# A two-layer hybrid decoder trunk: another order of chunks and engines, other first loads, smaller clears

## Chip, cores, metric

One Trainium2 chip, one core of it. The time is that of the whole kernel on the device in microseconds (us); a figure for a kernel is the median of its runs.

## What is computed

Two layers over 256 tokens of width 1024. One wide projection feeds two groups: HGRN2, a gated linear recurrence, and native sparse attention (compressed, selected and window keys). Their gated outputs go through `w_out`; then a second gated addition follows. The reference, cut:

```
for i in range(DEPTH):                                   # DEPTH = 2
    proj = rmsnorm(h, norm_g[i]) @ w_in[i]
    (hq, hf, hi, hgo, hz, nq, kcm, vcm, ksl, vsl, kwn, vwn, ngate, nz) = split(proj)
    log_f = logaddexp(log(lb), log1p(-lb) + log_sigmoid(hf)); k = (1 - lb) * sigmoid(-hf)
    o_hg  = rmsnorm(hgrn2(hq, log_f, k, hi))             # S_t = f_t S_(t-1) + k_t v_t; o_t = S_t q_t
    y_hg  = o_hg * sigmoid(hgo) * silu(hz)
    qn    = rmsnorm(nq)                                  # 8 heads of 64; q_rope = rope(qn)
    kc    = rmsnorm(compress(kcm)); vc = compress(vcm)   # 15 blocks of 32 tokens: silu(x @ w1) @ w2
    o_cmp = softmax(qn @ kc.T) @ vc
    o_slc = attention over the best selection blocks (4 blocks, all of them taken), k = rope(rmsnorm(ksl))
    o_win = window attention (window 512 over 256 tokens), k = rope(rmsnorm(kwn))
    y_nsa = (g0 * o_cmp + g1 * o_slc + g2 * o_win) * silu(nz)
    h = h + concat(y_hg, y_nsa) @ w_out[i]
    h = h + sigmoid(rmsnorm(h) @ w_pg[i]) * (p[i] @ w_pp[i])
```

## The kernel before

**Matrix products.** Every weight and every activation is split into a rounded part `hi` and a rest `lo`, and each product is three matmuls: hi by hi, hi by lo, lo by hi (`proj`, L581). A main matmul is 128x128 by 128x256; there are 2400. Weights come in chunks of 256 columns by 1024 rows, 1 MB each (the chunk `kk` has 280 columns), on SP's DMA queue (L426; ACT's queue L425 for the first two pieces) into four buffers `raw`. A chunk is cut into quarters: ACT casts `hi` (L534; for the first two chunks DVE may, L536), then DVE (L543) or GpSimd, called POOL (L544), subtracts for `lo`. A quarter is 128x512; nine pairs of such buffers exist. A chunk on PE is 48 main matmuls; its result lies in one of three PSUM banks `mm` (four more, `ax`, serve everything else, one, `po`, the attention sums) and is taken out by a function for each chunk (`ev_hf`, `ev_hi`, ...). The chunk names are those of the reference (`hf0`, `hf1` are the halves of hf, `cm` both compressed inputs, `kk` keys and gates, `vv` the values).

**Work beside the products.** The recurrence is a binary tree over time: elementwise scalings of tQ and tK on DVE and POOL (L420, L421), products by level on PE (L810 small levels, L870, L924), a masked copy L823 behind each L810, then L946 and L947. Compression (`ev_cm`): tqn (L991, L994), adds of the position term into PT (L420), the product with `w1` (L1022), an ACT step to t (L1028), L1037, then L1060 and L1061, L1067, L1092. Keys: roped by small steps of L420 or L421, scaled (POOL, L1246), rotated by a PE transposition (L1253), copied into tkh and tkl (L1261, L1264). Queries: L1131 to L1191, L1163 on PE. The softmax of the compressed keys: scores L1305, L1310 to L1344 on DVE, transposition L1351, result tPCh on ACT and tPCl on DVE (L1357), used by L1388. Attention runs in eight units a layer: scores L1426 and L1427, masked maximum on DVE (L1435), exponential on ACT (L1440), scaling on POOL (L1460), transposition on PE (L1477), copy on ACT (L1484) or DVE (L1481), sum L1402.

**Order.** No engine's order is written by hand. `Sched.run` is a greedy planner that runs when the kernel is built: all work is in threads; in each step the thread with the smallest start time plus `WGT[engine]` times its priority goes next. Priorities stand in `PRI`, the choice between engines (`alt`) is by the earlier end plus a bias in `PREF`, `STAY` lets PE stay with small products, durations are those written at each `op`, and `Port` marks DVE operations that the planner keeps apart from POOL's. What the chip does is then fixed: each engine runs its row in order and waits on semaphores.

The lines that the diff touches:

## Time and profile before

| | us |
|---|---|
| median of 3 runs | 386.61 (386.41 to 386.72) |
| profiled execution, its own time | 386.33 |
| its span in the trace | 384.4 |
| PE busy in the span | 375.0 |
| DVE busy | 310.5 |
| ACT busy | 260.6 |
| POOL busy | 114.0 |

The granted clock of PE is 0.999 over the span, 2.4 GHz. All engines run side by side; busy shares are means over a span whose stages differ, so the rows further down go by stage. Line numbers are those of the kernel before; in the changed kernel the same lines stand 5 to 8 lines further down (L543 is L548 there, L420 is L426, L924 is L932, L1028 is L1036, L1357 is L1365, L1426 is L1434).

### The profile page before, as it was taken

Reading aid. Unit: us, or ns where it says so; the run is one execution under the profiler, and the core shown is the slowest. Engines: PE = TensorE matmul, PEld = TensorE weight load, DVE = VectorE, ACT = ScalarE, POOL = GpSimd, SP = SyncE. Lnnn points to the kernel's source line nnn. Section 1 sums busy time; section 2 is a strip of 40 time slices with the busy share of each in tenths; the row PEclk is TensorE's granted clock in tenths of the full one; section 3 lists DMA queues with packets and bytes.
Section 4 is the critical chain, followed back from the end, with each engine's and each line's share of the span. In section 5 each row is a group of like instructions: output and inputs, shape, how many; then the busy total and the mean of one; then the engine's idle time right before and its main releaser. Section 6 shows DMA issues by size and latency. Waiting matters only on the chain.

```text
span 384.4 us, 9516 instructions
## 1 busy us (share of the span) xinstructions
PE 375.0 (98%) x3681; PEld 362.6 (94%) x3681; DVE 310.5 (81%) x791; ACT 260.6 (68%) x611; POOL 114.0 (30%) x135
## 2 busy tenths in 40 slices
...
GB/s 282 412 393 236 197 327 172 165 113 120 214 43 200 112 111 74 147 113 220 228 152 177 219 142 225 293 113 158 172 113 137 111 120 101 112 112 109 2 55 56
DMA packets 12286, 63.03 MB, mean 164 GB/s; under 512 B 1616, under 2 KB 2768, under 8 KB 5584
## 3 DMA queue, kind: packets, MB, share of 16 engines
...
HBM read 61.36 MB, written 1.05 MB: 162 GB/s over the span
## 4 chain that ended last, share of the span: by engine, by line
PE 75%; DVE 15%; DMA 5%; issue 2%; ACT 1%; POOL 0%; SPq 0%; POOLq 0%; ACTq 0%; DVEq 0%
PE mm L581 58%; DMA raw<-w_in 5%; PE po L1402 3%; PE mm L1612 3%; PE ax L1477 3%; DVE lo L543 3%; DVE PT L420 2%; PE ax L1426 2%; PE ax L810 1%; PE ax L1427 1%; DVE tK L420 1%; DVE tq L1191 1%; DVE tQ L420 1%; DVE t L1499 1%; PE po L1388 1%
## 5 line engine op out<-in xcount | busy, mean ns | idle before, releaser
L581 PE MATMUL mm<-xh,hi 128*128 128x256 f32 x608 | 175.5, 289 | 0.5 <-DVE hi L536 0.4
L581 PE MATMUL mm<-xl,hi 128*128 128x256 f32 x608 | 171.1, 281 | 0.0
L581 PE MATMUL mm<-xh,lo 128*128 128x256 f32 x608 | 170.6, 281 | 0.0
L534 ACT ACTIVATE hi<-raw 128x512 fp32r<-128x512 f32 (+1 forms) x203 | 123.4, 628 | 51.9 <-PE mm L581 38.3
L543 DVE TENSOR_TENSOR lo<-raw,hi 128x512 fp32r<-128x512 f32 (+2 forms) x183 | 125.7, 704 | 25.0 <-ACT hi L534 24.2
L581 PEld LDWEIGHTS mm<-xh,hi 128*128 128x128 f32 x608 | 114.4, 188 | 3.8 <-issue 1.4
L581 PEld LDWEIGHTS mm<-xh,lo 128*128 128x128 f32 x608 | 115.0, 189 | 0.4
L581 PEld LDWEIGHTS mm<-xl,hi 128*128 128x128 f32 x608 | 114.6, 188 | 0.4
L581 PE MATMUL mm<-hi,xh 128*128 128x256 f32 (+1 forms) x192 | 55.2, 288 | 0.0
L581 PE MATMUL mm<-lo,xh 128*128 128x256 f32 (+1 forms) x192 | 54.2, 282 | 0.2 <-DVE lo L543 0.2
L581 PE MATMUL mm<-hi,xl 128*128 128x256 f32 (+1 forms) x192 | 54.0, 281 | 0.0
L544 POOL TENSOR_TENSOR lo<-raw,hi 128x512 fp32r<-128x512 f32 x26 | 36.7, 1416 | 57.4 <-ACT hi L534 57.4
L1460 POOL TENSOR_SCALAR P<-P,s 128x128 f32<-128x128 f32 (+1 forms) x64 | 38.6, 618 | 34.3 <-DVE s L1453 18.5
L581 PEld LDWEIGHTS mm<-lo,xh 128*128 128x128 f32 x192 | 36.1, 188 | 0.4 <-DVE lo L543 0.4
L581 PEld LDWEIGHTS mm<-hi,xh 128*128 128x128 f32 x192 | 36.1, 188 | 0.4
L581 PEld LDWEIGHTS mm<-hi,xl 128*128 128x128 f32 x192 | 36.2, 188 | 0.0
L1440 ACT ACTIVATE P<-P,s 128x128 f32<-128x128 f32 (+1 forms) x64 | 28.3, 445 | 0.9 <-DVE s L1435 0.9
L1435 DVE CUSTOM_DVE_ANT_0 P<-ax,cn 128x128 f32<-128x128 f32 (+1 forms) x64 | 20.0, 351 | 4.2 <-PE ax L1427 3.2
L630 POOL TENSOR_TENSOR s<-s,mhalf 128x2 f32<-128x2 f32 x4 | 3.8, 946 | 55.8 <-DVE s L626 55.8
L1484 ACT ACTIVATE PT<-ax 128x512 f32<-128x512 f32 x24 | 14.0, 596 | 3.2 <-PE ax L1477 3.1
L1227 POOL TENSOR_TENSOR s<-s,mhalf 128x4 f32<-128x4 f32 x4 | 4.4, 1110 | 38.7 <-DVE s L1223 38.7
L1477 PE MATMUL ax<-cn,P 128*128 128x128 f32 x96 | 13.9, 272 | 0.0
...
## 6 DMA issues: line engine op xcount, KB each, us to landing
...
```

The source lines that it names most:

```text
L420: return alt([("V", dV2(n), lambda: V.tensor_tensor(out, in0, in1, op=fn), 0.0), ("G", dG2(n), lambda: G.tensor_tensor(out, in0, in1, op=f ...
L534: ("S", dS(m), lambda: S.activation(hi, src, AF.Copy), 0.0)]
L543: yield alt([("V", dV2(m), lambda: V.tensor_tensor(lo, src, hv, op=OP.subtract), 0.0), ("G", dG2(m), lambda: G.tensor_tensor(lo, src, hv, ...
L544: ("G", dG2(m), lambda: G.tensor_tensor(lo, src, hv, op=OP.subtract), PREF["lo_G"])],
L581: PE.matmul(out, lhsT=a, rhs=b, start=k == 0 and i == 0 and (j == 0 or nb == 2), stop=k == NK - 1 and i == 2, skip_group_check=True)
L1402: PE.matmul(po.ap[64 * par:64 * par + 64, tt * 128:(tt + 1) * 128], lhsT=vn[:, st, b, par], rhs=PTs[tt][par][b * (tt + 1) + st], start=Fal ...
L1435: yield op("V", dV(ns) + 0.02, lambda: V.tensor_tensor_reduce(P[:, b], sv[:, b], cn[:, CN_CA + 128 - ns + 128:CN_CA + 256], -1.0, 3.0e38, ...
L1440: yield op("S", Act("exp", dS(ns, 2)), lambda: S.activation(P[:, b], P[:, b], AF.Exp, bias=nm.ap[:, b:b + 1], scale=-1.0, accum_out=sm_.ap ...
L1460: ("G", dG(ns) + 0.05, lambda: G.tensor_scalar(P[:, b], P[:, b], w, 1.0, op0=OP.mult, op1=OP.mult), PREF["P_G"]),
L1477: PE.transpose(tb.ap[:, i * 128:(i + 1) * 128], Ps[par][1][:, b, st * 128:(st + 1) * 128], idf)
L1484: ("S", dS(w_), lambda: S.activation(PT.ap[:, 0:w_], tb.ap[:, 0:w_], AF.Copy), PREF["PT_S"])],
L1612: PE.matmul(out, lhsT=x[:, k, w], rhs=y[:, t], start=k == 0 and i == 0, stop=k == 1 and i == 2)
```

## The change

Four things change at once.

1. The planner's numbers: order of the chunks, `WGT`, `PREF`, `PRI`, `STAY`, the place of `w1` in the loads (behind the eighth chunk, not the fifth) and some durations. Tables are now kept for each layer, with equal entries. The arithmetic stays the same.
2. The clears of the five PT buffers cover only the columns 30 and 31 of each 32, not all 512.
3. The first loads: the small columns `sm` leave the first load of `h` and go on ACT's queue; of the first two weight pieces only the second stays on ACT's queue.
4. `lo` and other steps that two engines may do land elsewhere, since the bias is another.

```diff
-ORDER = ["hf0", "hi1", "hi0", "hq0", "kk", "cm", "hf1", "hq1", "nq0", "hgo0", "nq1", "vv", "hz0", "hz1", "nz1",
-         "hgo1", "nz0"]
+ORDER = [["hi0", "hi1", "hf0", "hq0", "kk", "cm", "hf1", "hq1", "nq0", "hgo0", "nq1", "hz0", "vv", "hz1",
+          "hgo1", "nz0", "nz1"],
...
-PREF = dict(hi_G=3.8, lo_G=-0.3, acc_G=7.2, t2_G=0.1, P_G=-2.3, P_S=1.4, PT_S=-2.4, hi_V=-0.4)
+PREF = [dict(hi_G=2.5, lo_G=0.4, acc_G=6.4, t2_G=0.0, P_G=-0.7, P_S=1.9, PT_S=-3.1, hi_V=-0.3),
...
-BUFS = dict(mm=3, ax=4, raw=4, w1=4, t5=3, P=4, PT=5, t2=2, au=3, hl=9, wt=9)
+BUFS = dict(mm=3, ax=4, raw=4, w1=7, t5=3, P=4, PT=5, t2=2, au=3, hl=9, wt=9)
...
-        G.memset(b.ap, 0.0)
+        G.memset(b.ap.rearrange("p (j m) -> p j m", j=16)[:, :, 30:32], 0.0)
...
         def x(k, n):
-            lo = SM_N + k * T if k else 0
-            hi_ = SM_N + (k + n) * T
-            yield dma(hs[:, lo:hi_], xs[:, lo:hi_], (hi_ - lo) * 0.5, ht[k:k + n] + ([] if k else [smt[0]]),
-                      {2: 1.0, 4: 0.6}.get(k, 0.0))
+            lo, hi_ = SM_N + k * T, SM_N + (k + n) * T
+            yield dma(hs[:, lo:hi_], xs[:, lo:hi_], (hi_ - lo) * 0.5, ht[k:k + n], {2: 0.7, 4: 0.4}.get(k, 0.0))
...
         yield from x(0, 1)
-        pa, pb = pieces(items[0], (1, 1, 2, 2, 2), 2), pieces(items[1], (2, 2, 2, 2))
+        yield dma(hs[:, 0:SM_N], xs[:, 0:SM_N], 51, [smt[0]], act=True)
+        pa, pb = pieces(items[0], (1, 1, 2, 2, 2), (1,)), pieces(items[1], (2, 2, 2, 2))
...
-            yield dma(b.ap[:, a], src[:, a], nk * n * 0.5, b.t[k:k + nk], act=k < na)
+            yield dma(b.ap[:, a], src[:, a], nk * n * 0.5, b.t[k:k + nk], act=k in na)
```

**What moves on the engines.** The numbers of instructions of each kind stay the same but for the engine that does them: DVE's splits of 128x512 (L543) go from 173 to 194, POOL's (L544) from 26 to 5; DVE's casts of that size (L536) from 4 to 2, ACT's (L534) from 195 to 197. Four scalings of the tree's totals go from DVE to POOL, and of the key ropes' small steps one goes to DVE.

Places on PE, counted in main matmuls issued ahead of them:

| step | before | after |
|---|---|---|
| layer 0: first L1022 / L1037 | 336 / 354 | 336 / 354 |
| L1060 and the second L1253 | 378 | 372 |
| L1305 | 612 | 600 |
| L870, 32 rows / 64 rows | 612 / 636 | 612 / 672 |
| L1351 | 678 | 672 |
| first L924 | 672 | 702 |
| first L1426 | 678 | 708 |
| last L1402 | 900 | 882 |
| layer 1: L1022 / L1037 | 1530 / 1548 | 1536 / 1554 |
| the second L1253 | 1578 | 1584 |
| first L924 / first L1426 | 1872 / 1878 | 1902 / 1908 |

POOL at the compression of layer 0, before. In front of the rows is a scaling of the statistics; `md`, `t` are buffers of the key rope.

```order
L1227 TENSOR_TENSOR s_142<-s_141,mhalf 128x4
L1246 TENSOR_SCALAR t_0_114<-t_2_116 128x512
L544 TENSOR_TENSOR lo_88<-raw_96,hi_87 128x512
L544 TENSOR_TENSOR lo_90<-raw_96,hi_89 128x512
L544 TENSOR_TENSOR lo_92<-raw_96,hi_91 128x512
L544 TENSOR_TENSOR lo_94<-raw_96,hi_93 128x512
L1227 TENSOR_TENSOR s_144<-s_143,mhalf 128x4
L421 TENSOR_TENSOR t_0_114<-md_136 128x2x8 x2
L1246 TENSOR_SCALAR t_1_115<-t_0_114 128x512
```

The same place after:

```order
L1235 TENSOR_TENSOR s_142<-s_141,mhalf 128x4
L427 TENSOR_TENSOR t_2_116<-md_136 128x2x8
L1254 TENSOR_SCALAR t_0_114<-t_2_116 128x512
L549 TENSOR_TENSOR lo_88<-raw_95,hi_87 128x512
L549 TENSOR_TENSOR lo_78<-raw_98,hi_77 128x512
L1235 TENSOR_TENSOR s_144<-s_143,mhalf 128x4
L1254 TENSOR_SCALAR t_1_115<-t_0_114 128x512
```

Two of four splits have left this place, and both small rope steps of the second key half are now DVE's.

ACT at the same stage, before: `gt` the gates, `tF` and `tG` the decay's two parts, the last row the compression's step L1028.

```order
L1212 ACTIVATE gt_157<-mm_63,s_140 128x24
L1216 ACTIVATE t_0_114<-mm_63 128x256
L534 ACTIVATE hi_77<-raw_98 128x512
L729 ACTIVATE tF_99<-t_1_115 128x512
L731 ACTIVATE tG_100<-t_1_115 128x512
L1028 ACTIVATE t_2_116<-ax_69 128x256
```

After:

```order
L539 ACTIVATE hi_77<-raw_98 128x512
L1220 ACTIVATE gt_157<-mm_65,s_140 128x24
L1224 ACTIVATE t_0_114<-mm_65 128x256
L737 ACTIVATE tF_99<-t_1_115 128x512
L1036 ACTIVATE t_2_116<-ax_69 128x256
L739 ACTIVATE tG_100<-t_1_115 128x512
```

The compression's step and tG have changed places.

DVE at the end of the tree of layer 0, before; `s` and `md` belong to the softmax of the compressed keys, the two rows with tot_134 are the tree's last scalings, on which L924 waits.

```order
L420 TENSOR_TENSOR tQ<-tQ,tot_134 128x4x64
L1336 TENSOR_REDUCE s_150<-md_137 128x16
L420 TENSOR_TENSOR tK_101<-tK_101,tot_134 128x4x64
L1337 TENSOR_SCALAR s_150<-s_150 128x16
L543 TENSOR_TENSOR lo_92<-raw_96,hi_91 128x512
L1338 RECIPROCAL s_150<-s_150 128x16
L543 TENSOR_TENSOR lo_94<-raw_96,hi_93 128x512
L1342 TENSOR_TENSOR s_150<-s_150,gt_157 128x16
L543 TENSOR_TENSOR lo_78<-raw_96,hi_77 128x512
L1344 TENSOR_TENSOR md_137<-md_137,s_150 128x240
L543 TENSOR_TENSOR lo_80<-raw_95,hi_79 128x512
```

After, from the same softmax step (L1342 is L1350 there):

```order
L1350 TENSOR_TENSOR s_150<-s_150,gt_157 128x16
L548 TENSOR_TENSOR lo_88<-raw_96,hi_87 128x512
L1352 TENSOR_TENSOR md_137<-md_137,s_150 128x240
L548 TENSOR_TENSOR lo_90<-raw_95,hi_89 128x512
L548 TENSOR_TENSOR lo_92<-raw_95,hi_91 128x512
L548 TENSOR_TENSOR lo_94<-raw_95,hi_93 128x512
L548 TENSOR_TENSOR lo_78<-raw_95,hi_77 128x512
L548 TENSOR_TENSOR lo_80<-raw_97,hi_79 128x512
L1365 TENSOR_TENSOR tPCl<-ax_69,tPCh 120x256
L426 TENSOR_TENSOR tQ<-tQ,tot_134 128x4x64
L426 TENSOR_TENSOR tK_101<-tK_101,tot_134 128x4x64
```

The last scalings stand behind that softmax, six splits and tPCl. Between the masked copy L823 of the second product L810 and the last scaling of tK, DVE has 11 splits before and 19 after. From the first L1440 to the last L1484 of layer 0, ACT has 21 casts before and 17 after.

## Rows read from the trace of the kernel before

**Rows 1.** The page's first part: busy time in us, share of the span, and instructions of an engine.

```profile
PE 375.0 (98%) x3681; PEld 362.6 (94%) x3681; DVE 310.5 (81%) x791; ACT 260.6 (68%) x611; POOL 114.0 (30%) x135
```

**Rows 2.** The chain of work that ended last, in order of time, at the start: start and length in us, and what. The first row is the load of kk.

```profile
15.30 6.97 DMA raw<-w_in
22.35 0.67 ACT hi L534
23.02 0.74 ACT tV L774 x2
23.80 16.22 PE mm L581 x131
```

**Rows 3.** Busy time of each engine in one stretch, 12 to 23 us (its bounds and length first; then PE, PE's weight loads, DVE, ACT and POOL, instructions in brackets), with PE's granted clock, the busy share of the DMA engines and what they moved.

```profile
12.00:23.00 11.00, 11.00 (x96) 11.00 (x95) 10.34 (x29) 7.93 (x19) 0.71 (x1) 1.00 1.05 410
```

**Rows 4.** The timeline of PE around the compression of layer 0: start, length, engine, line, operation, tiles, count, and in brackets the idle time before it and what ended it.

```profile
47.12 0.28 PE L581 MATMUL mm<-xh,hi 128*128 128x256 f32 x1
47.23 0.28 PE L581 MATMUL mm<-xl,hi 128*128 128x256 f32 x1
47.36 0.28 PE L581 MATMUL mm<-xh,lo 128*128 128x256 f32 x1
47.56 1.08 PE L1022 MATMUL ax<-raw,PT 128*32 128x128 f32 x32
49.33 1.08 PE L1022 MATMUL ax<-raw,PT 128*32 128x128 f32 x32 [0.69 <-DVE PT L420]
50.34 0.39 PE L581 MATMUL mm<-xh,hi 128*128 128x256 f32 x1
50.57 0.28 PE L581 MATMUL mm<-xl,hi 128*128 128x256 f32 x1
...
53.25 0.63 PE L1037 MATMUL ax<-cn,t 128*128 128x32 f32 x4 [0.53 <-ACT t L1028]
```

**Rows 5.** The timeline at the first scores, of layer 0 and of layer 1 (PE).

```profile
104.67 0.39 PE L1426 MATMUL ax<-tkh,tq 128*128 128x256 f32 x1 [0.67 <-DVE tPCl L1357]
...
291.95 0.39 PE L1426 MATMUL ax<-tkh,tq 128*128 128x256 f32 x1 [0.68 <-DVE tPCl L1357]
```

**Rows 6.** The timeline at the second rotation of keys in layer 1 (DVE, POOL, PE).

```profile
242.40 1.28 DVE L543 TENSOR_TENSOR lo<-raw,hi 128x512 fp32r<-128x512 f32 x2
242.41 1.76 POOL L1246 TENSOR_SCALAR t<-t 128x512 f32<-128x512 f32 x1 [1.03 <-PE ax L1061]
...
244.22 0.66 PE L1253 MATMUL ax<-cn,t 128*128 128x128 f32 x4 [1.16 <-POOL t L1246]
```

**Rows 7.** The chain that ended last again, from the compression of layer 0 to that of layer 1, and one pair of DVE splits later in it.

```profile
45.22 4.32 DVE PT L420 x8
...
52.32 0.62 ACT tG L731
...
232.32 2.89 DVE PT L420 x7
...
264.45 1.20 DVE lo L543 x2
```

**Rows 8.** The timeline of the first 6 us (POOL and DVE).

```profile
1.86 2.38 POOL L416 MEMSET PT<- 128x512 f32 x5
...
3.68 0.70 DVE L536 CAST hi<-raw 128x256 fp32r<-128x256 f32 x1 [2.73 <-DMA raw<-w_in]
...
5.03 0.28 DVE L536 CAST hi<-raw 128x256 fp32r<-128x256 f32 x1
```

**Rows 9.** The view of one source line, of POOL's splits and of DVE's: shortest, median and longest in ns, first and last start, and the forms.

```profile
L544 POOL TENSOR_TENSOR lo<-raw,hi x26: 1282/1317/1965, 42.9 to 355.5; 128x512 fp32r<-128x512 f32 x26
...
L543 DVE TENSOR_TENSOR lo<-raw,hi x183: 410/684/1264, 4.7 to 368.4; 128x512 fp32r<-128x512 f32 x173, 128x560 fp32r<-128x560 f32 x8, 128x256 fp32r<-128x256 f32 x2
```

**Rows 10.** The timeline of POOL, DVE and PE in the tree of layer 0.

```profile
85.87 1.32 POOL L544 TENSOR_TENSOR lo<-raw,hi 128x512 fp32r<-128x512 f32 x1
...
86.33 1.41 DVE L420 TENSOR_TENSOR tK<-tK,tot 128x512 f32<-128x512 f32 x1
...
88.26 0.68 DVE L420 TENSOR_TENSOR tK<-tK,tot 128x512 f32<-128x512 f32 x1
...
98.95 0.41 DVE L420 TENSOR_TENSOR tK<-tK,tot 128x256 f32<-128x256 f32 x1
...
99.71 1.06 PE L924 MATMUL ax<-tQ,tK 128*128 128x128 f32 x8
```

**Rows 11.** The timeline of POOL beside the compression of layer 0, and one row of it in layer 1.

```profile
42.04 0.91 POOL L1246 TENSOR_SCALAR t<-t 128x512 f32<-128x512 f32 x1 [4.09 <-DVE t L420]
42.92 2.57 POOL L544 TENSOR_TENSOR lo<-raw,hi 128x512 fp32r<-128x512 f32 x2
45.92 2.69 POOL L544 TENSOR_TENSOR lo<-raw,hi 128x512 fp32r<-128x512 f32 x2 [0.43 <-ACT hi L534]
...
233.13 1.39 POOL L544 TENSOR_TENSOR lo<-raw,hi 128x512 fp32r<-128x512 f32 x1 [2.29 <-ACT hi L534]
```

**Rows 12.** Busy time in three stretches of layer 0, with the columns of rows 3: the second half of the tree, attention, and what follows.

```profile
71.30:99.40 28.10, 28.10 (x334) 27.32 (x335) 26.35 (x66) 19.28 (x39) 8.29 (x7) 1.00 0.44 151
104.20:157.00 52.80, 52.33 (x470) 50.25 (x472) 36.91 (x133) 45.00 (x132) 27.31 (x39) 1.00 0.33 117
157.00:210.00 53.00, 53.00 (x453) 52.81 (x450) 46.95 (x97) 37.18 (x78) 3.86 (x3) 1.00 0.51 181
```

More of the change, by code (lines that the diff above doesn't have):

```diff
@@ L27 @@
     0, 128, 384, 640, 880, 912, 920, 952, 984
-ORDER = ["hf0", "hi1", "hi0", "hq0", "kk", "cm", "hf1", "hq1", "nq0", "hgo0", "nq1", "vv", "hz0", "hz1", "nz1",
-         "hgo1", "nz0"]
+ORDER = [["hi0", "hi1", "hf0", "hq0", "kk", "cm", "hf1", "hq1", "nq0", "hgo0", "nq1", "hz0", "vv", "hz1",
+          "hgo1", "nz0", "nz1"],
+         ["hi0", "hi1", "hf0", "hq0", "kk", "cm", "hf1", "hq1", "nq0", "hgo0", "nq1", "hz0", "vv", "hz1",
+          "hgo1", "nz0", "nz1"]]
 LAT = {"P": 0.2, "S": 0.146, "V": 0.125, "G": 0.08, "D": 0.0}
-WGT = {"P": 0.0289, "S": 0.3304, "V": 0.0174, "G": 0.0122, "D": 0.02}
-PREF = dict(hi_G=3.8, lo_G=-0.3, acc_G=7.2, t2_G=0.1, P_G=-2.3, P_S=1.4, PT_S=-2.4, hi_V=-0.4)
+WGT = {"P": 0.0646, "S": 0.3093, "V": 0.048, "G": 0.0028, "D": 0.02}
+PREF = [dict(hi_G=2.5, lo_G=0.4, acc_G=6.4, t2_G=0.0, P_G=-0.7, P_S=1.9, PT_S=-3.1, hi_V=-0.3),
+        dict(hi_G=2.5, lo_G=0.4, acc_G=6.4, t2_G=0.0, P_G=-0.7, P_S=1.9, PT_S=-3.1, hi_V=-0.3)]
 MARG = {"P": 1.25, "S": 0, "V": 0, "G": 0, "D": 0.0}
 WAR = 0.15
-STAY = 7.5
+STAY = 8.7
 SWITCH = {"rt": 0.0, "tr": 0.085, "tt": 0.08, "rc": 0.095, "tc": 0.095, "cr": 0.21, "ct": 0.19}
 HELD = 0.1
-PRI = dict(st=92, small=18, ropes=260, tree=88, hgrn=57, csm=10, att=76, att_step=9, unit=17, split=154, lo=133,
-           ld2=24, proj=145, pp=74, w_out=166, w_pg=213, hf=120, hq=144, hi=75, cm=11, nq=7, kk=26, vv=230,
-           hz=65, hgo=241, nz=55, out=0, pg=331, tab=119)
-BUFS = dict(mm=3, ax=4, raw=4, w1=4, t5=3, P=4, PT=5, t2=2, au=3, hl=9, wt=9)
+PRI = [dict(st=46, small=8, ropes=264, tree=151, hgrn=27, csm=34, att=59, att_step=10, unit=0, split=174,
+            lo=158, ld2=102, proj=160, pp=92, w_out=156, w_pg=201, hf=117, hq=216, hi=87, cm=12, nq=55, kk=48,
+            vv=257, hz=126, hgo=282, nz=128, out=24, pg=284, tab=228),
+       dict(st=46, small=8, ropes=264, tree=151, hgrn=27, csm=34, att=59, att_step=10, unit=0, split=174,
+            lo=158, ld2=102, proj=160, pp=92, w_out=156, w_pg=201, hf=117, hq=216, hi=87, cm=12, nq=55, kk=48,
+            vv=257, hz=126, hgo=282, nz=128, out=24, pg=284, tab=228)]
+BUFS = dict(mm=3, ax=4, raw=4, w1=7, t5=3, P=4, PT=5, t2=2, au=3, hl=9, wt=9)
 def in_groups():
@@ L72, in in_groups @@
     ch = dict(ch)
-    return [(n, ch[n]) for n in ORDER]
+    return [[(n, ch[n]) for n in o] for o in ORDER]
 CHUNKS = in_groups()
@@ L428, in trunk @@
     woff, o = {}, 0
-    for name, cols in CHUNKS:
+    for name, cols in CHUNKS[0]:
         woff[name] = (o, len(cols))
@@ L433, in trunk @@
     for l in range(L):
-        for i, (name, _) in enumerate(CHUNKS):
+        for i, (name, _) in enumerate(CHUNKS[l]):
             o, n = woff[name]
@@ L1662, in ple @@
             Y = yield wait(e("Y"))
-            for c in range(len(CHUNKS)):
-                yield wait(sch.e("hl", (l, CHUNKS[c][0]), 3))
+            for c in range(len(CHUNKS[l])):
+                yield wait(sch.e("hl", (l, CHUNKS[l][c][0]), 3))
             yield wait(e("xdone"))
@@ L1738, in xdone @@
         def xdone():
-            for name, _ in CHUNKS:
+            for name, _ in CHUNKS[l]:
                 k, c = (name[:-1], int(name[-1])) if name[-1] in "01" else (name, 0)
```

92 lines of the change are left out of this document (47 added, 45 removed).

## The prediction

> **What bounds the kernel now.** I read the page's engine shares first. TensorE (PE) is busy 375.0 of 384.4 us, 98%, VectorE (DVE) 81%, ScalarE (ACT) 68% [rows 1]. So a change can gain only where PE stands still or starts later than it need; all other speed is cover. Then I read the chain that ended last for what PE waited on, and the timeline around each wait for its size. In the timeline an idle mark is taken from a modelled end: a main matmul shows 0.28 us but the next issues 0.12 us behind it (starts at 47.12, 47.23, 47.36 [rows 4]), so the real gap in the issue is the idle mark plus 0.16.
>
> The first 23.8 us: the load of kk, the fifth chunk, is issued at 15.30 and lands at 22.3, ACT casts it in 0.67, then evacuates tV in 0.74, which frees a PSUM bank, and PE goes on at 23.80 [rows 2]. From 12 to 23 us the DMA engines are busy at a share of 1.05 with 410 GB/s [rows 3].
>
> After that PE really stops at five places. Compression (L1022, L1037) of layer 0: idle 0.69 for the DVE adds into PT and 0.53 for ACT's t, real 0.85 and 0.69 [rows 4]. The first scores L1426 of layer 0 and of layer 1: idle 0.67 and 0.68 behind tPCl, real 0.83 and 0.84 [rows 5]. The rotated keys L1253 of layer 1: idle 1.16 behind POOL's t of L1246, real 1.32 [rows 6]. Sum 0.85 + 0.69 + 0.83 + 0.84 + 1.32 = 4.53 us. In layer 1 the chain also runs through the adds into PT [rows 7], so L1022 waited for them, though no idle mark shows; I put up to 0.3 there. Everything this change can win inside the kernel is these 4.8 us.
>
> **The change part by part.** The sum is made against the profiled execution's own 386.33 us. The median shown, 386.61, stands 0.28 above it.
>
> *Start.* The five memsets of PT take 2.38 us of GpSimd (POOL) up to 4.24 now; of 128x512 they become 128x32 elements. Beside them the first cast on DVE takes 0.70, its twin at 5.03 only 0.28 [rows 8]. So 0.42 can come out of the path to the first matmul. The small columns leave the first SP load, the second weight piece stays on ACT's queue, the first goes to SP. What is lost at the other end: PE ends this head start at the bank that tV frees, and tV stands behind the cast of kk in ACT's row in both kernels. The bytes ahead of kk are the same in both, and the DMA engines are full up to its landing. The cover for "nothing" is therefore the kk load; without it the gain is 0.42. Bounds -0.4 to +0.3 (a DMA order that lands kk one cast of 0.3 later); I take 0.
>
> *Splits go from POOL to DVE.* DVE's 128x512 splits go from 173 to 194, POOL's from 26 to 5. A split costs POOL 1.32 (median), DVE 0.60 in a row (two in the chain take 1.20) [rows 7, 9]. So 21 x 0.60 = 12.6 us more of DVE's time over both layers, and less of what POOL's splits do to DVE: beside the POOL split at 85.87 the product tK takes 1.41, the next one 0.68, so this split cost DVE 0.73 [rows 10]. The Trainium skill ("Perfetto Trace Analysis", section "Optimizing Scalar/DVE Operations") says that DVE and GpSimd share a read port, held as a lock, so that moving operations between those two might not help; taken at its word, each moved split costs DVE nothing net, and this is the second rival below. The row agrees for that one split; most POOL splits show no such neighbour, so I do not count the whole back.
>
> *Compression, layer 0 (-1.0).* Four POOL splits lie in 42.92 to 48.6, two of them beside the PT adds [rows 11]; the new row has two behind the rotation and none of the later pair. The eight PT adds take 4.32 here; in layer 1 seven, with one POOL split beside them, take 2.89, which is 3.30 for eight [rows 7, 11]. So about 1.0 comes off the adds, against a stop of 0.85. One DVE split (0.60) now stands directly ahead of them, but five other rows less. On ACT t (now L1036) moves ahead of tG, which is 0.62 [rows 7] against a stop of 0.69. Bounds -1.54 (both stops gone) to 0 (the DVE split and later arrival eat them); value -1.0, nearer the two matching rows.
>
> *Compression and keys, layer 1 (-1.1).* L1022, L1037 and the second L1253 each stand 6 main matmuls later on PE, 6 x 0.12 = 0.7 us. POOL's t takes 1.76 at 242.41, with two DVE splits of 1.28 beside it [rows 6], and 0.91 in layer 0 [rows 11]. With 0.7 less to wait and up to 0.85 less in POOL, 1.32 is covered if the sides fall well. Bounds -1.6 to 0; value -1.1 (0.7 for the place, and the rest of the 1.32 and the 0.3 at half).
>
> *Tree and first scores (-0.3 in each layer).* The first L1426 moves from 678 to 708 main matmuls of its layer, 30 x 0.12 = 3.6 us later, while tPCl moves ahead of tQ and tK on DVE. Its stop of 0.83 goes. In its place stand two new waits, for L924 and for L1351: between the second product of the tree (L823 behind the second L810, 71.3) and the last tK DVE now has 19 splits instead of 11, 8 x 0.60 = 4.8 us. Back come the 0.73 of the port [rows 10] and two small POOL moves of 0.2 together. So tK is 3.9 later, and L924, 30 main matmuls later, wants it 3.6 later: 0.3 short. Today tK is done at 99.36 and L924 issues at 99.71 [rows 10], 0.35 of slack. That is just even; since L1351 stands 6 matmuls (0.7 us) earlier than before while its softmax steps share DVE with the same eight splits, I count 0.5 of new wait. -0.83 + 0.5 = -0.3. Bounds -0.83 (no new wait) to +0.7 (nothing comes back from POOL, 4.8 - 3.6 - 0.35 = 0.85, and L1351 waits its full 0.7 on top: 1.55 - 0.83).
>
> *Attention (+0.3 in each layer).* From the first L1426 to the last L1402 PE has 174 main matmuls to fill with instead of 222: 48 x 0.12 = 5.7 us less cover. ACT is busy 45.00 of 52.80 there, 85% [rows 12], and loses 4 casts of 0.61, so it must do 42.6 in 47.1, 90%. PE shows no stop there today. Bounds 0 to +2.9 (if ACT cannot go above its 85%: 42.6 / 0.852 = 50.0 against 47.1); I take 0.3, near today's zero, because the units already run without a PE stop at 85%. Of the 48 matmuls taken out 30 stand in front, in the tree, where they pay for the DVE splits, and 18 behind. ACT's four casts fall into 157 to 210, where it is busy 37.18 of 53 [rows 12].
>
> *Switches of matmul kind (+0.4).* L1305 and the 32-row products of L870 shared one break in the row of main matmuls and now stand apart, and so do two more small groups in each layer. Going in costs 0.20 instead of 0.12 (47.36 to 47.56), coming out 0.23 (50.34 to 50.57) [rows 4]: 0.19 for one break, 2 layers x 1 to 2 of them, 0.4 to 0.8, less where L924 and L1351 join others. Bounds 0 to 0.8, value 0.4.
>
> The later chunks' new order (hz0 before vv, nz0 before nz1), w1 loaded after hq1, the per-layer tables and the changed durations of the planner change no instruction's cost; splits run some microseconds ahead of PE, so I count 0.
>
> Sum: 0 - 1.0 - 1.1 - 0.6 + 0.6 + 0.4 = -1.7, 386.33 - 1.7 = 384.6; with the 0.28, **384.9 us** as a median.
>
> **The rivals.** (1) *The head start is kept.* If kk lands 0.4 earlier, PE resumes earlier by that: 384.9 - 0.4 = 384.5. For it: POOL's memsets really go. Against: the 1.05 share. (2) *The port gives everything back.* A POOL split blocks DVE for more than the 0.60 that DVE needs itself, as in that row (0.73) [rows 10]. Then tK is not late, the two 0.5 of new waits go, and both stops of 0.83 are won in full: 384.9 - 1.0 = 383.9; with the rest of the compression stops too (another 1.0) 382.9. If every stop went and no break was added, 386.61 - 4.8 = 381.8. (3) *The waits only change their names.* L932 and L1359 take over what L1426 gave, and PE arrives early at compression: the cm terms at half (-1.0), tree 0, attention +0.6, breaks +0.4: 386.6. For it: DVE is at 26.35 of 28.10 in the tree [rows 12], with no room for eight splits. (4) *Slower: ACT bounds the attention.* Place: from the first L1434 to the last L1410. Price: it decides from 1.15 a layer on (0.85 more than the 0.3, twice, eats the -1.7) and ends at 2.9; in the middle, 2.0, the sum is -1.7 + 3.4 = +1.7, with the 0.28 388.3. For it: 90% needed where 85% is seen, at a chain of exponentials, scalings and transposes; against: PE has no stop there now.
>
> **How the numbers follow.** Forecast 0.44 (383.9 to 385.9), rival 1 0.10, rival 2 0.11, rival 3 0.19, rival 4 0.16. About 0.2% (0.8 us) is what a measurement of this kernel can tell from no change, so faster is below 385.8. Faster: 0.44 less 0.03 of its upper end, plus 0.21, 0.62. Same: 0.19 of rival 3 with 0.03 from the forecast, less 0.03 that falls above, 0.19. Slower: rival 4 and that rest, 0.19. The range leaves out the far end of rival 2 (0.05), and the upper part of rivals 3 and 4 (0.1): 382.4 to 388.2.
>
> **What would show it.** Right: PE's second matmul stretch still begins near 23.8; no idle mark at L1045 behind ACT, at L1261 behind POOL; none over 0.2 at the first L1434 behind tPCl; small marks at L932 and L1359; the last L1410 of a layer some 2 us earlier than 157.3. Wrong: a stop at L932 of more than 0.7 (the eight splits are not paid for), idle marks at L1410 or the transposes behind ACT of more than 1.2 a layer (rival 4), or a start that ends earlier than 23.5 (rival 1). The step I trust least is the new wait at L932 and L1359, a difference of large numbers.

## The result and the profile after

The changed kernel takes 382.70 us as a median (382.45 to 383.03, 5 runs), the kernel before 386.46 (386.33 to 386.72, 5 runs): ratio 0.9902, 95% interval 0.9887 to 0.9916. That is faster by 3.8 us, 1.0%. The forecast was 384.9, faster by 1.7. The sign and the range hold the result; the gain is more than twice what was forecast.

The page's first part of the changed kernel, to be read beside [rows 1]: PE loses only 0.7 us of busy time, the span loses 4.0, POOL goes from 114.0 to 78.6, DVE gains 1.0.

```profile
PE 374.3 (98%) x3681; PEld 361.9 (95%) x3681; DVE 311.5 (82%) x805; ACT 261.3 (69%) x613; POOL 78.6 (21%) x119
```

So no work was saved on PE; waits went. And DVE is busy only 1.0 us more with 21 more splits, where the forecast had charged 12.6 for them. The page's shares of the chain that ended last say the same, for the changed kernel and then for the one before: what was 15% DVE and 5% DMA is PE now.

```profile
PE 96%; DMA 1%; DVE 1%; SPq 0%; issue 0%; ACT 0%; DVEq 0%
```

```profile
PE 75%; DVE 15%; DMA 5%; issue 2%; ACT 1%; POOL 0%; SPq 0%; POOLq 0%; ACTq 0%; DVEq 0%
```

Where in the program? Four points have the same number of main matmuls ahead of them in both kernels (144, 474, 1056 and 1674): PE's restart behind tV, the second L810 (now L818) of layer 0, a run of 24 in the gate part of layer 0, and the second L810 of layer 1. The chain of work of the changed kernel gives their starts (start, length, what):

```profile
24.71 20.61 PE mm L586 x168
...
69.56 1.03 PE ax L818 x64
...
174.63 2.94 PE mm L586 x24
...
254.21 1.03 PE ax L818 x64
```

and that of the kernel before (the first point is in [rows 2], 23.80):

```profile
70.23 1.03 PE ax L810 x64
...
176.31 2.94 PE mm L581 x24
...
257.52 1.07 PE ax L810 x64
```

The difference from point to point is what each stage gained or lost; the last row runs to the end of the spans, 384.4 and 380.4.

| stage | before to after, at its end | change in it | forecast |
|---|---|---|---|
| start, to the 144th main matmul | 23.80, 24.71 | +0.91 | 0 |
| layer 0: compression, keys | 70.23, 69.56 | -1.58 | -1.0 |
| layer 0: rest of tree, scores, attention | 176.31, 174.63 | -1.01 | +0.2 (-0.3 + 0.3 + 0.2) |
| layer 1: compression, keys | 257.52, 254.21 | -1.63 | -1.1 |
| layer 1: the rest | 384.4, 380.4 | -0.69 | +0.2 |
| sum | | -4.00 | -1.7 |

(Executions carry some 2 us beside the span; the two profiled ones differ by 386.33 - 382.45 = 3.88.) All five stops are gone: L1030, L1045, L1261 and L1434 (L1022, L1037, L1253, L1426 before) show no idle time ahead of them in any layer, and neither do L932 and L1359, where the forecast had put new waits. The start got worse, which the forecast had at nothing.

The timeline at the places of [rows 4, 5, 7, 10, 11] in the changed kernel (DVE, POOL and PE):

```profile
45.37 0.69 DVE L548 TENSOR_TENSOR lo<-raw,hi 128x512 fp32r<-128x512 f32 x1
45.98 2.27 DVE L426 TENSOR_TENSOR PT<-tqn,h 128x120 f32<-128x120 f32 x8
...
240.33 0.93 POOL L1254 TENSOR_SCALAR t<-t 128x512 f32<-128x512 f32 x1 [2.33 <-DVE t L426]
...
97.76 0.40 DVE L1352 TENSOR_TENSOR md<-md,s 128x240 f32<-128x240 f32 x1
...
99.14 0.43 PE L1359 MATMUL ax<-cn,md 128*120 128x128 f32 x2
...
101.21 0.43 DVE L1365 TENSOR_TENSOR tPCl<-ax,tPCh 120x256 fp32r<-120x256 f32 x1
...
101.88 0.42 DVE L426 TENSOR_TENSOR tK<-tK,tot 128x256 f32<-128x256 f32 x1
...
102.95 1.05 PE L932 MATMUL ax<-tQ,tK 128*128 128x128 f32 x8
...
106.50 0.28 PE L1434 MATMUL ax<-tkh,tq 128*128 128x256 f32 x1
```

Eight PT adds take 2.27 us where they took 4.32: no POOL split stands beside them any more. POOL's t of layer 1 takes 0.93 where it took 1.76. The softmax step L1352, which L1359 needs, is done at 98.16, and L1359 issues at 99.14: 0.98 us of slack. The last tK is done at 102.30 and L932 issues at 102.95: 0.65 us of slack, where there was 0.35. tPCl is done at 101.64, and the score matmul that stopped before, the third L1434, comes at 106.50, 4.9 us behind it.

Busy time in the second part of the tree and in attention (from the first L1434 to the last L1410 of layer 0; the columns are those of rows 3), beside [rows 12]:

```profile
71.00:102.90 31.90, 31.90 (x367) 30.76 (x366) 30.96 (x75) 22.05 (x43) 4.66 (x6) 1.00 0.41 144
105.80:153.60 47.80, 47.80 (x434) 45.44 (x432) 35.60 (x133) 42.44 (x129) 19.27 (x34) 1.00 0.34 117
```

DVE is busy 30.96 of 31.90 us in the tree, so it does run with no room there; but PE never waits for it. In attention ACT is busy 42.44 of 47.80, 89%, close to the 42.6 of 47.1 in the forecast, and PE is busy all of it. The work was forecast rightly; that it would cost PE 0.3 a layer was not.

### The profile page after: what moved, and what is told of

Same layout as the page of the kernel before. It is cut to its first block, busy times and chain, and to the rows that moved or that the text cites. A ratio compares the mean times of both kernels' runs of the same rounds, so it can differ in the third digit from the quotient of the medians.

```text
span 380.4 us, 9523 instructions
## 1 busy us (share of the span) xinstructions
PE 374.3 (98%) x3681; PEld 361.9 (95%) x3681; DVE 311.5 (82%) x805; ACT 261.3 (69%) x613; POOL 78.6 (21%) x119
## 3 DMA queue, kind: packets, MB, share of 16 engines
HBM read 61.36 MB, written 1.05 MB: 164 GB/s over the span
## 4 chain that ended last, share of the span: by engine, by line
PE 96%; DMA 1%; DVE 1%; SPq 0%; issue 0%; ACT 0%; DVEq 0%
PE mm L586 75%; PE po L1410 3%; PE ax L1485 3%; PE mm L1620 3%; PE ax L1434 2%; PE ax L818 2%; PE ax L1435 1%; DMA raw<-w_in 1%; PE ax L1030 1%; PE ax L955 1%; PE ax L1171 1%; PE po L1396 1%; PE ax L878 1%; PE ax L954 0%; PE ax L932 0%; PE ax L1261 0%
## 5 line engine op out<-in xcount | busy, mean ns | idle before, releaser
L548 DVE TENSOR_TENSOR lo<-raw,hi 128x512 fp32r<-128x512 f32 (+2 forms) x204 | 136.4, 690 | 29.2 <-ACT hi L539 27.9
L1468 POOL TENSOR_SCALAR P<-P,s 128x128 f32<-128x128 f32 (+1 forms) x64 | 34.8, 558 | 29.4 <-PE mm L1620 12.2
L1485 PE MATMUL ax<-cn,P 128*128 128x128 f32 x96 | 14.6, 274 | 0.0
L617 ACT ACTIVATE t<-h 128x256 f32<-128x256 f32 x28 | 11.2, 405 | 3.3 <-DVE h L1713 3.1
```

Of the source, the lines that this page charges most:

```text
L548: yield alt([("V", dV2(m), lambda: V.tensor_tensor(lo, src, hv, op=OP.subtract), 0.0), ("G", dG2(m), lambda: G.tensor_tensor(lo, src, hv, ...
L617: yield op("S", dS(T), lambda: S.activation(b.ap, h[:, k], AF.Square), [ht[k]], b.t)
L1468: ("G", dG(ns) + 0.05, lambda: G.tensor_scalar(P[:, b], P[:, b], w, 1.0, op0=OP.mult, op1=OP.mult), PREF[l]["P_G"]),
L1485: PE.transpose(tb.ap[:, i * 128:(i + 1) * 128], Ps[par][1][:, b, st * 128:(st + 1) * 128], idf)
```

## The experiments

All but the two kernels themselves are played back: the planner's order of one kernel is written down step by step, engine and buffer included, and given out again with only the named steps changed. Every other row of every engine stays as it is, so one part is tested alone, which an edit of the planner's numbers can't do. The lines of these kernels stand 56 to 58 further down. Each was compared with runs of the kernel before on its own chip (medians 386.5 to 386.8), so ratios are what to compare; differences below are ratio times 386.5.

### The start

Edit of `a_loads0`, on the changed kernel:

```diff
-            lo, hi_ = SM_N + k * T, SM_N + (k + n) * T
+            lo = SM_N + k * T if k else 0
+            hi_ = SM_N + (k + n) * T
...
-        yield dma(hs[:, 0:SM_N], xs[:, 0:SM_N], 51, [smt[0]], act=True)
-        pa, pb = pieces(items[0], (1, 1, 2, 2, 2), (1,)), pieces(items[1], (2, 2, 2, 2))
+        pa, pb = pieces(items[0], (1, 1, 2, 2, 2), (0, 1)), pieces(items[1], (2, 2, 2, 2))
```

> The changed kernel, every engine's row kept as it is, with the first loads of before (small columns with the first rows of h on SP, both first weight pieces on ACT's queue). In the changed kernel the 24th main matmul issues at 9.42 us, before at 8.55, and PE keeps that loss of 0.95 us up to the 288th. Theory Q (the first weight piece on SP's queue pushes every later SP load back by one issue, 0.45 us): 382.7 - 0.9 = 381.8. Theory S (the separate load of the small columns costs it): the same, 381.8. Theory O (the loads are innocent, the new chunk order and the casts on ACT cost it): 382.7, no change.

Measured: 381.94 us (381.77 to 383.06), ratio 0.9881 (0.9866 to 0.9897): 0.8 faster than the changed kernel. The intervals of the two ratios overlap, but the traces tell them apart: the 144th main matmul issues at 23.88 instead of 24.71, and from there to the end of the span both take the same, 355.79 and 355.72.

`b_loads1` is the same edit the other way round, on the kernel before:

```diff
-        pa, pb = pieces(items[0], (1, 1, 2, 2, 2), 2), pieces(items[1], (2, 2, 2, 2))
+        yield dma(hs[:, 0:SM_N], xs[:, 0:SM_N], 51, [smt[0]], act=True)
+        pa, pb = pieces(items[0], (1, 1, 2, 2, 2), (1,)), pieces(items[1], (2, 2, 2, 2))
```

> The kernel before, every engine's row kept, with the first loads of the changed one. Theories Q and S: the same loss as in the changed kernel, less the 0.3 that PE waits at 23.4 us before: 386.5 + 0.6 to 0.95 = 387.1 to 387.4. Theory O, and the forecast's step that PE's start is evened out at 23.8 us anyway: 386.5.

Measured: 387.45 us (386.98 to 388.29), ratio 1.0026 (1.0016 to 1.0036): slower by 1.0. So the loads alone cost 0.8 to 1.0 us in either order, and theory O falls. The forecast's step that PE's start evens out at the bank of tV does not fall with it: as the rows further down show, PE still restarts there, but later.

`a_w0act` and `a_smSP` part the two edits of the loads:

```diff
-        pa, pb = pieces(items[0], (1, 1, 2, 2, 2), (1,)), pieces(items[1], (2, 2, 2, 2))
+        pa, pb = pieces(items[0], (1, 1, 2, 2, 2), (0, 1)), pieces(items[1], (2, 2, 2, 2))
```

> The changed kernel, every engine's row kept, but the first weight piece goes back to ACT's queue, behind the small columns, which stay a load of their own there. Theory Q: all or most of the 0.9 us comes back, about 381.9. Theory S: nothing comes back, 382.6 to 382.8. Theory O: 382.7.

Measured: 383.41 us (382.70 to 384.62), ratio 0.9916 (0.9898 to 0.9934). Nothing comes back by the times, which speaks against theory Q; the trace, further down, does not.

`a_smSP` has that line and also:

```diff
-        yield dma(hs[:, 0:SM_N], xs[:, 0:SM_N], 51, [smt[0]], act=True)
+        yield dma(hs[:, 0:SM_N], xs[:, 0:SM_N], 51, [smt[0]])
```

> The changed kernel with another start: the small columns still a load of their own, but on SP's queue behind the first rows of h, and both first weight pieces on ACT's queue, as before. Theory S (a separate load of 128 short rows costs the DMA engines the 0.9 us wherever it stands): 382.6 to 383.0. Theory W (what costs is that the small columns stand ahead of the first weight pieces on ACT's queue): 381.9.

Measured: 382.85 us (382.29 to 383.16), ratio 0.9899 (0.9886 to 0.9912), the same as the changed kernel; theory W falls. What the slower starts share is that the DMA engines move less at the outset. The stretch from 4 to 6 us, in the order before, changed, a_loads0, a_smSP, b_loads1 (last column GB/s):

```profile
4.00:6.00 2.00, 1.61 (x9) 1.26 (x8) 2.00 (x7) 0.53 (x3) 0.24 (x1) 1.00 1.00 354
```

```profile
4.00:6.00 2.00, 1.67 (x9) 1.10 (x8) 1.91 (x6) 0.51 (x1) 0.00 (x0) 1.00 0.82 209
```

```profile
4.00:6.00 2.00, 1.45 (x9) 0.99 (x8) 1.94 (x7) 1.29 (x4) 0.00 (x0) 1.00 1.03 376
```

```profile
4.00:6.00 2.00, 1.47 (x5) 1.03 (x5) 1.03 (x4) 0.86 (x2) 0.00 (x0) 1.00 0.88 258
```

```profile
4.00:6.00 2.00, 1.62 (x7) 1.42 (x7) 1.71 (x5) 0.51 (x1) 0.23 (x1) 1.00 0.91 228
```

With the first loads of before the queues move 354 and 376 GB/s there, with those of the other three 209, 258 and 228. The first 6 us of the kernel before and of the changed one:

```profile
0.00:6.00 6.00, 4.64 (x15) 2.14 (x15) 2.46 (x10) 2.52 (x5) 3.71 (x11) 1.00 0.70 231
```

```profile
0.00:6.00 6.00, 4.69 (x15) 1.99 (x15) 2.10 (x9) 2.50 (x4) 1.68 (x11) 1.00 0.65 171
```

The changed kernel has moved 0.36 MB less by then, which at the 410 GB/s of [rows 3] is 0.88 us (an estimate). From 6 to 22 us the DMA engines are busy at a share of 1.04 and 1.05, so what is lost is not made up, and kk lands later by about that much. ACT's cast of kk and its steps tV, in the changed kernel, in `a_loads0` and in `a_w0act` (before: 22.35 and 23.02 in [rows 2]):

```profile
23.26 0.67 ACT L539 ACTIVATE hi<-raw 128x560 fp32r<-128x560 f32 x1 [2.12 <-DMA raw<-w_in]
23.84 1.55 ACT L782 ACTIVATE tV<-mm,s 128x256 f32<-128x256 f32 x4
```

```profile
22.43 0.67 ACT L597 ACTIVATE hi<-raw 128x560 fp32r<-128x560 f32 x1 [2.15 <-DMA raw<-w_in]
23.00 1.55 ACT L840 ACTIVATE tV<-mm,s 128x256 f32<-128x256 f32 x4
```

```profile
22.49 0.67 ACT L596 ACTIVATE hi<-raw 128x560 fp32r<-128x560 f32 x1 [1.98 <-DMA raw<-w_in]
24.46 1.57 ACT L839 ACTIVATE tV<-mm,s 128x256 f32<-128x256 f32 x4 [1.30 <-DVE s L754]
```

The second step of tV ends at 24.66 in the changed kernel, at 23.82 in `a_loads0` and at 23.75 before, and PE's 144th main matmul issues 0.05 or 0.06 behind it in all three. So the bank of tV does set PE's restart, and it is kk that comes 0.91 later.

Which of the two edits costs the rate? The runs with a late kk have one more load on SP's queue ahead of the third weight piece: the first weight piece, or in `a_smSP` the small columns. That piece is issued at 2.08 to 2.10 there and at 1.62 or 1.63 in the others. In the seven traces of this kind, those of the next two sections among them, the cast of kk begins at 22.99 to 23.73, in the six others at 22.35 to 22.71. `a_w0act` is one of the six: it has the separate load of the small columns, moves 334 GB/s at 4 to 6 us and casts kk at 22.49. So theory Q fits the traces if it is taken for any further load on SP's queue, and theory S does not; but where they part this rests on the one trace of `a_w0act`, and its time shows no gain. The Trainium skill ("DMA: Bandwidth & Descriptors", section "Specifications") names 512 bytes as the least for a transfer at full rate; the rows of the small columns, 128 of 408 bytes, are below that, but `a_w0act` has the same load, so no run here shows that they cost the rate. In `a_w0act` something else came on top. PE stood idle until 7.05, and its granted clock (third column from the right in the stretches) then shows 0.86 and 0.50, the 1.2 GHz level, in which main matmuls issue 0.21 apart instead of 0.12. PE's timeline and the stretches of 7 to 9 us:

```profile
7.05 0.36 PE L643 MATMUL mm<-hi,xh 128*128 128x256 f32 x1 [0.85 <-ACT hi L596]
...
8.29 0.42 PE L643 MATMUL mm<-hi,xh 128*128 128x256 f32 x1
8.50 0.42 PE L643 MATMUL mm<-lo,xh 128*128 128x256 f32 x1
```

```profile
7.00:8.00 1.00, 0.67 (x2) 0.50 (x3) 1.00 (x3) 0.92 (x4) 0.00 (x0) 0.86 0.99 375
8.00:9.00 1.00, 1.00 (x6) 1.00 (x6) 1.00 (x4) 0.54 (x2) 0.00 (x0) 0.50 1.09 406
```

So the late start of that trace is not the cost of the loads alone.

Five other traces begin at that level, with either kind of loads: where PE does not wait, main matmuls issue 0.21 apart up to 9.17 us in `a_smSP`, 10.17 in `b_loads1`, 9.1 in `a_tG`, 8.7 in `b_loV` and 10.4 in `b_rows_loV`, and 0.12 apart from there on. (The stretches print 1.00 before that too, but these traces have no clock entry so early.) PE in `b_rows_loV`, which has the loads of the kernel before:

```profile
9.53 0.41 PE L638 MATMUL mm<-lo,xh 128*128 128x256 f32 x1
9.74 0.41 PE L638 MATMUL mm<-hi,xl 128*128 128x256 f32 x1
...
10.38 0.28 PE L638 MATMUL mm<-hi,xl 128*128 128x256 f32 x1
10.50 0.28 PE L638 MATMUL mm<-xh,hi 128*128 128x256 f32 x1
```

In `a_smSP` and `a_tG` this costs nothing, since PE waits for tV at the 144th main matmul in any case (25.18, 24.72). In `b_loV`, `b_loads1` and `b_rows_loV` PE reaches it behind tV, at 24.14, 25.10 and 25.16; so a late start in a single trace of these is not the loads' alone. (In `b_loads1` the second step of tV ends at 24.79, 1.04 later than before: so much of its 1.30 comes with kk.)

`a_clear0` puts the full clears back:

```diff
-        G.memset(b.ap.rearrange("p (j m) -> p j m", j=16)[:, :, 30:32], 0.0)
+        G.memset(b.ap, 0.0)
```

> The changed kernel with the five full clears of PT (128x512) again, nothing else. If the clears hold up the first cast on DVE as read in the trace of before (0.70 against 0.28) and PE's start is set by that: 382.7 + 0.4 = 383.1. If the landing of the first weights sets it, 382.7.

Measured: 382.93 us, ratio 0.9897 (0.9881 to 0.9912), from three executions; the fourth, the profiled one, took 1286.29 us and is left out, so there is no trace to read. By the times the smaller clears bring nothing that can be measured; an effect of 0.4 us would lie within the interval.

### Splits on POOL or on DVE

`b_loV`: the order before, with 26 rows moved between engines in place:

```diff
-POOL L544 TENSOR_TENSOR lo<-raw,hi 128x512   (all 26)
+DVE  L543 TENSOR_TENSOR lo<-raw,hi 128x512   (at the same step)
```

> The kernel before, every engine's row kept, but all 26 of POOL's splits done by DVE at the same place in the order. Theory P (a POOL split holds up DVE for about as long as DVE would need for it): DVE gets no later, the stop of 0.85 us behind the PT adds of layer 0 falls, 386.5 - 0.5 to 0.9 = 385.6 to 386.0. Theory R (the forecast: most POOL splits cost DVE nothing, each moved one costs DVE 0.60): the scalings before L924 and tPCl come later, the stops there grow by about 1 us a layer, 387.0 to 388.5.

Measured: 387.89 us (387.59 to 388.30), ratio 1.0032 (1.0021 to 1.0044): slower by 1.2. Its trace is 0.34 late at the 144th main matmul (the low level at the start) and loses 1.06 behind it. Theory R, the forecast's, is right for this order. The stop behind the PT adds is gone, but three others come or grow. PE's timeline (L981 is L924, L1483 is L1426, L1310 is L1253):

```profile
100.58 1.13 PE L981 MATMUL ax<-tQ,tK 128*128 128x128 f32 x8 [0.34 <-DVE s L1394]
...
105.73 0.39 PE L1483 MATMUL ax<-tkh,tq 128*128 128x256 f32 x1 [0.80 <-DVE tPCl L1414]
...
57.28 0.66 PE L1310 MATMUL ax<-cn,t 128*128 128x128 f32 x4 [0.45 <-POOL t L1303]
```

L924 now waits 0.34 by its idle mark (0.50 in the issue), just the 0.5 that the forecast charged; the score stop grows from 0.67 to 0.80, and the keys' rotation in layer 0 waits 0.45.

But the price of a moved split was too high even here. The page's first part of `b_loV` (DVE was busy 310.5 before):

```profile
PE 376.1 (97%) x3681; PEld 364.2 (94%) x3681; DVE 317.2 (82%) x817; ACT 261.1 (68%) x611; POOL 78.4 (20%) x109
```

26 splits at 0.60 are 15.6 us, and DVE is busy 6.7 longer: 8.9 came back, because POOL's splits no longer hold it up. In the trace of the kernel before, 16 of the 26 POOL splits stand beside a DVE instruction that takes over 0.1 us longer than its like, 9.1 us in all, where the forecast saw none beside most of them. What decides is not the sum but the place.

`a_loG` is the opposite, on the changed kernel: the 24 quarters that only before were POOL's go back. `a_loG_cm` takes only those at compression and keys (6), `a_loG_att` only those in attention (8):

```diff
-DVE  L548 TENSOR_TENSOR lo<-raw,hi 128x512   (24, 6 or 8)
+POOL L549 TENSOR_TENSOR lo<-raw,hi 128x512   (at the same step)
```

> The changed kernel, every engine's row kept, but the quarters that POOL split in the kernel before (24 of them, the same chunks and quarters) go back to POOL; its own 5 stay there. Theory P: DVE is held up again, some stops come back (L1030 behind PT first), 382.7 + 0.4 to 1.5 = 383.1 to 384.2. Theory R: DVE gains room, nothing is later, 382.4 to 382.7.

> The changed kernel, every engine's row kept, but six splits back on POOL: the quarters that POOL split beside compression and key ropes in the kernel before (nq0 quarters 1 to 3 in layer 0; four are named in layer 1, three of them are DVE's now). Theory P (POOL's splits there hold up the PT adds and L1254): the adds into PT go from 2.27 us for eight toward 4.3, stops come back at L1030 and at the second rotation, 382.7 + 0.6 to 1.5 = 383.3 to 384.2. Theory C (the stops are covered by the new places on PE alone): 382.7.

> The changed kernel, every engine's row kept, but the eight splits of pp and w_out that POOL had during attention go back to POOL. If POOL's splits delay its own scaling of P (L1468) and DVE there, the attention stretches get longer, as the 24 splits together made them by 0.9 and 0.4 us: 382.7 + 0.5 to 1.3 = 383.2 to 384.0. If the loss of the 24 lies in compression and keys alone: 382.7.

Measured: `a_loG` 385.65 us (384.95 to 386.04), ratio 0.9968 (0.9953 to 0.9983), 2.6 slower than the changed kernel's 0.9902; `a_loG_cm` 384.16, ratio 0.9941 (0.9926 to 0.9955), 1.5 slower; `a_loG_att` 384.08, ratio 0.9935 (0.9922 to 0.9947), 1.3 slower. So in the new order the move to DVE is worth 2.6 us, in the old one it costs 1.2. From the 144th main matmul on, where the noise of the start is left out, the traces give 3.05, 1.66 and 1.54: the other ten of the 24 quarters cost nothing that can be told. Of the 4.92 that the changed kernel gains behind that point, 1.87 stays with the splits back on POOL; that is the worth of the order with its new places on PE, which no run takes apart further. Theory P holds where a POOL split has a neighbour that matters. The timeline of `a_loG_cm` at the PT adds of both layers (POOL, DVE, POOL, DVE; L606 is L549, L483 is L426):

```profile
42.93 4.14 POOL L606 TENSOR_TENSOR lo<-raw,hi 128x512 fp32r<-128x512 f32 x3
47.48 1.38 POOL L606 TENSOR_TENSOR lo<-raw,hi 128x512 fp32r<-128x512 f32 x1 [0.42 <-ACT hi L596]
...
45.05 4.50 DVE L483 TENSOR_TENSOR PT<-tqn,h 128x120 f32<-128x120 f32 x8
...
230.99 1.29 POOL L606 TENSOR_TENSOR lo<-raw,hi 128x512 fp32r<-128x512 f32 x1 [1.40 <-ACT hi L596]
...
231.02 3.30 DVE L483 TENSOR_TENSOR PT<-tqn,sm 128x120 f32<-128x120 f32 x8
```

Eight adds: 2.27 us with no split beside them, 3.30 with one, 4.50 with two and the tail of a third. One by one, an add takes 0.35, the one that meets a POOL split 1.33 to 1.41, and it ends 0.14 to 0.16 behind the split; the tail costs 0.26. So one POOL split of 1.29 to 1.43 costs DVE 1.0 there. The Trainium skill ("SBUF — State Buffer", section "SBUF: two separate sides") has the shared port as a lock that one of the two engines holds for a whole instruction while the other stands; these adds agree with that. PE takes 0.74 us longer in the compression stage of layer 0 than in the changed kernel, and 0.61 longer in that of layer 1. In attention the largest single wait is for POOL's own scaling of P, which comes late behind a split: 0.50 in the issue, of 0.8 lost in layer 0; what makes up the 0.8 in layer 1 shows no mark and was not followed. PE's timeline of `a_loG_att` has the one mark (L1542 is L1485, L1525 is L1468):

```profile
146.86 0.33 PE L1542 MATMUL ax<-cn,P 128*128 128x128 f32 x1 [0.33 <-POOL P L1525]
```

### Single rows by hand

`b_rows`: in the kernel before, two rows moved by hand, the compression's step in layer 0 and tPCl in both layers:

```diff
-ACT  tG L731;  t L1028
+ACT  t L1028;  tG L731
...
-DVE  tQ L1517;  tQ L1541;  t L1499;  tPCl L1357
+DVE  tQ L1517;  tPCl L1357;  tQ L1541;  t L1499
```

> The kernel before with two moves by hand: ACT does the compression's step L1028 ahead of tG in layer 0, and DVE does tPCl (L1357) ahead of two of the three gate steps in front of it in both layers. Nothing else. Theory N (each stop hangs on the one row ahead of it): the stops of 0.69, 0.83 and 0.84 go, 386.5 - 2.3 = 384.2. Theory M (the forecast: behind a stop the next late thing stands close, half of it or less is won): 385.4 to 386.

> Both at once: the two hand moves and all 26 splits on DVE, in the order of before. Theories P and N together: 384.2 - 0.5 to 0.9 = 383.3 to 383.7, without any of the new places on PE. Theory R: no better than the hand moves alone, 384.2 or more.

Measured: `b_rows` 386.04 us (385.55 to 386.49), ratio 0.9982 (0.9973 to 0.9991), 0.7 faster; `b_rows_loV` 387.07 us (386.49 to 387.44), ratio 1.0007 (0.9998 to 1.0017), no better than before. (The trace of `b_rows_loV` loses 1.36 at its start, at the low level, and is 0.14 ahead of the kernel before behind the 144th main matmul; `b_rows` is 0.37 ahead there. So the 26 moves bring nothing on top of the hand moves, as theory R says.) Theory N falls: three stops of together 2.4 us go, and 0.7 is won. In layer 0 the four POOL splits now run in one row beside the PT adds, and the stop that was taken from L1037 turns up at L1022 (L1079 here):

```profile
43.48 5.19 POOL L601 TENSOR_TENSOR lo<-raw,hi 128x512 fp32r<-128x512 f32 x4
...
48.87 1.38 PE L1079 MATMUL ax<-raw,PT 128*32 128x128 f32 x36 [1.06 <-DVE PT L477]
```

The score stops, 0.83 and 0.84, are gone (the largest excess over the usual issue at a score matmul is 0.22), yet some 0.5 of each is given back in attention: from the 690th to the 708th main matmul PE takes 3.72 us instead of 3.19, from the 1890th to the 1920th 7.01 instead of 6.49 (counted in the traces). In the old order the waits do move on, as the forecast's third rival has it.

`a_tG` tests one of these rows in the new order:

```diff
-ACT  t L1036;  tG L739      (both layers)
+ACT  tG L739;  t L1036
```

> The changed kernel with one pair of ACT steps swapped back in each layer: tG ahead of the compression's step L1036, as before. If that order was what removed the stop at L1045 (0.69 us in layer 0): 382.7 + 0.4 to 0.7 = 383.1 to 383.4. If the earlier end of the PT adds is enough by itself: 382.7.

Measured: 382.63 us (382.31 to 383.10), ratio 0.9896 (0.9883 to 0.9909): no change. The ACT rows and PE's answer (L1093 is L1036, L1102 is L1045):

```profile
51.53 0.61 ACT L796 ACTIVATE tG<-t 128x512 f32<-128x512 f32 x1
52.06 0.36 ACT L1093 ACTIVATE t<-ax 128x256 f32<-128x256 f32 x1
...
52.60 0.53 PE L1102 MATMUL ax<-cn,t 128*128 128x32 f32 x4
```

t is done at 52.42, L1045 wants it at 52.60. The swap on ACT, to which the forecast gave 0.62 against a stop of 0.69, was not needed: with the PT adds 2.05 shorter everything behind them was early enough.

## Why the prediction was wrong

The mechanism was right: PE's stops are what there was to win, and they are what was won. The size was off by 2.3 us, and the working shows where.

**The costs set against the stops, +2.0, were not there.** This is the step that failed. The sum carried +0.5 of new wait at L924 and L1351 and +0.3 for attention in each layer, and +0.4 for breaks. With them the two rest stages came to +0.4, although both score stops were counted as won; measured is -1.70 (-1.01 and -0.69), about the two score stops of 0.83 and 0.84 with no cost against them. The new wait: DVE and L924 were worked out to come out even, and did (0.65 of slack). The 0.5 was put there because L1351's softmax steps "share DVE with the same eight splits"; but in the new order five of the splits and the last scalings stand behind the last of these steps, and L1359 had 0.98 of slack. The price of the splits was wrong as well: "most POOL splits show no such neighbour" does not hold, and of the 12.6 us charged to DVE 1.0 shows in its busy time (the casts and small scalings that left DVE hide some 1.7 us more). `b_loV` shows that such a wait is real when the splits come without the 30 main matmuls of delay on PE: 0.50 there. Attention: ACT at 89% held up nobody. (The stretch that the forecast read begins at 104.20, not with the first L1426, which issues at 102.34; from there to 157.30 ACT is busy 46.17 of 54.96, and the share needed comes out at 89% again.) Breaks: I counted those that come apart and not those that join; in the traces the row of main matmuls is broken 77 times after and 89 times before, and the two score stops account for the rest stages without any cost of breaks.

**Compression and keys, -2.1, were -3.2.** This term was too small by 1.1. The saving on the PT adds was put at 1.0, from a row of layer 1 that itself has one POOL split beside it. With none it is 2.05; the shortest of these adds in the view of their source line, 339 ns against a longest of 1368, would have told so. With that everything behind is early, and both stops of layer 0 went whole; in layer 1 all of the 1.32 and the 0.3 went. `a_loG_cm` shows the part of the splits in this: 0.74 and 0.61 of the two stages, 1.35 of the 3.2.

**The start, 0, was +0.9**, outside its bounds of -0.4 to +0.3. The bound of +0.3 was for kk landing late; it was much later, 0.91. That PE's head start ends at the bank of tV was right; what failed is the premise that the DMA engines are full up to the landing of kk. At 4 to 6 us they moved 209 GB/s instead of 354, so the same bytes were through later, and PE restarts at 24.71, not 23.80. The clears did what was read from the rows: the first cast on DVE takes 0.29 instead of 0.70, and PE's first main matmul issues at 4.39 instead of 4.53; behind the bank of tV nothing of that is left, as forecast, and the times of `a_clear0` show nothing of it.

**The rivals.** The second, with every stop gone and part of the costs gone, comes nearest in time (382.9 and 381.8); but its reason, that the port gives back every moved split, is not general: in the old order 26 moved splits still add 6.7 us to DVE's busy time, and the kernel loses 1.2. The third holds in the old order (`b_rows`) and not in the new one. Neither the ACT-bound attention nor the kept head start showed up.

**What beats both kernels** is `a_loads0`, the changed kernel with the old first loads: ratio 0.9881 against 0.9902. The two intervals overlap; that the loads are the difference rests on the traces of the two, which differ only ahead of the 144th main matmul, and on the times of `b_loads1`.

What stays open: whether one more load on SP's queue by itself costs the 0.8, as the traces have it, and why so much; what brings PE up to the full clock so late in five of the traces; and which places of the new order make up its 1.87.
